# A fifth room for raw expert weights, and a first norm whose sums come from the residual operation and from ScalarE

## Chip, cores and metric

The kernel runs on one core of a Trainium2 chip. The metric is device time in microseconds (us) of one execution; the time of a kernel is the median of its runs. An execution was also taken by the hardware profiler, and the rows below are from it. DVE is VectorE, ACT is ScalarE, POOL is GpSimd, PE is TensorE's matmul, PEld its weight load, SP the SyncE queue that issues most transfers.

## What is computed

One layer of a decoder over 2048 tokens of width 1024. The part that matters here:

```
x = layer_norm(ALPHA * x + g1 * (mixed @ w_out), ln_mix_g, ln_mix_b)      # the first norm
h = x * (1 + sc2) + sh2
scores = sigmoid(h @ router_w); 8 of 64 experts are chosen for each token
y = sum over the chosen experts e of gate * (silu(h @ w1[e]) * (h @ w3[e])) @ w2[e]  + a shared expert
x = layer_norm(ALPHA * x + g2 * y, ln_ffn_g, ln_ffn_b)
layer_norm: (x - mean) * rsqrt(mean((x - mean)^2) + 1e-5) * g + b
```

`mixed` is made by three token mixers (a recurrent one and two kinds of attention) that take the first half of the time.

## The kernel before, in words

The program is written as tiles in pools. A pool has a number of rooms (`bufs`) for each tile name; a tile that is made when all rooms are taken waits until the oldest one's last reader is done. The order of the instructions on each engine is fixed when the program is built, by a scheduler that goes by the order in the source, by priorities and by its own planned times; on the chip each engine's queue runs in that order, and semaphores hold an instruction until what it needs is there.

**Phase C (`phase_c`, the first norm and the routing).** 16 blocks of 128 tokens go through `tile_`. For each block the mixed rows are multiplied by w_out in two halves of 512 columns (48 matmuls, L1836). DVE adds the residual (`scalar_tensor_tensor`, L1837) into `r` and takes statistics of each half (`bn_stats`, L1840). `layer_norm_hat` joins them (`bn_aggr`, L1996), adds the epsilon (L1998), takes the reciprocal root in eleven small DVE operations (L711 to L716), makes the bias (L2001), and ACT writes the normalised rows (L2004). DVE then makes `h2` (L1845) and `h2p` (L1849, read by PE for the router, L1860 and L1865) and the scaled rows that are kept (L1851, L1852). `route` works out the chosen experts of four or two blocks at a time, on DVE, in pieces put between the blocks; after the last block `rank_experts` sorts the experts by their load.

**Experts (`moe_phase`).** Work goes unit by unit: three units of the shared expert, then the 64 experts in the order largest, smallest, second largest and so on, each in groups of up to 320 tokens, then the shared expert again with the second norm. Expert weights come in as six raw tiles `wraw` of 128x1024 (512 KB each) an expert: SP loads one into a room of pool `e_wr` (four rooms, L2055), ACT copies it to the high part (L2059), DVE subtracts to get the low part (L2060), which frees the room. High and low parts lie in ten rooms of 8 KB (`e_ws`). PE runs the hidden matmuls (L2093 for small groups, L2112 for large ones), the way back (L2129), transposes of the gathered tokens (L2072) and small matmuls that find token numbers (L2194). These last two share three PSUM rooms named `tr` (L2072's are freed by L65, L2194's by the small DVE operations L2202 and L2203, and the transposes of L2103 in small groups by L65 again). POOL gathers tokens (L2140) and adds results to memory (L2166) by indirect transfers.

Of the kernel before, what the change touches and what calls it, by code (L numbers as in the profile page):

```python
# [6 lines left out]
F32 = mybir.dt.float32  # L7
# [5 lines left out]
AF = mybir.ActivationFunctionType  # L13
ALU = mybir.AluOpType
AX = mybir.AxisListType
PSUM = bass.MemoryType.PSUM
P = 128
T = 2048
D = 1024
# [9 lines left out]
ALPHA = 2.0 ** 0.25  # L29
# [673 lines left out]
def rsqrt(nc, pool, x, shape, floor=None, name="rs"):  # L703

    V = nc.vector
    if floor is not None:
        V.tensor_scalar(x, x, floor, None, op0=ALU.max)
    t = pool.tile(shape, I32, name=name + "i")
    y = pool.tile(shape, F32, name=name + "y")
    a = pool.tile(shape, F32, name=name + "a")  # L710
    V.tensor_scalar(t, x.bitcast(I32), 1, None, op0=ALU.logical_shift_right)  # L711
    V.tensor_scalar(y.bitcast(I32), t, -1.0, float(0x5f3759df), op0=ALU.mult, op1=ALU.add)  # L712
    for _ in range(3):
        V.scalar_tensor_tensor(a, y, -0.5, y, op0=ALU.mult, op1=ALU.mult)  # L714
        V.tensor_tensor(a, a, x, op=ALU.mult)  # L715
        V.scalar_tensor_tensor(y, a, 1.5, y, op0=ALU.add, op1=ALU.mult)  # L716
    return y
# [848 lines left out]
def mixed(nc, S, pool, t, res, queue, lo_eng):  # L1566

    m = pool.tile([P, KT, P], F32, name="m")
    queue.dma_start(m, S["mixT"].rearrange("(k p) t -> p k t", p=P)[:, :, t * P:(t + 1) * P])
    yield  # L1570
    mH = pool.tile([P, KT, P], F32R, name="mH")
    mL = pool.tile([P, KT, P], F32R, name="mL")
    split_to(nc, mH, mL, m, lo_eng=lo_eng)
    res += [mH, mL]
    yield
# [179 lines left out]
def phase_c(tc, A, g, S, mixT, modrow, C):  # L1755


    nc = tc.nc
    V, G, ACT, PE = nc.vector, nc.gpsimd, nc.scalar, nc.tensor
    woH, woL = C.wo  # L1760
    with ExitStack() as es:
# [3 lines left out]
        wk = pool("c_wk", 2)  # L1765
# [13 lines left out]
        sm = pool("c_sm", 1)  # L1779
# [36 lines left out]
        mv = mixT.rearrange("(k p) t -> p k t", p=P)  # L1816

        def tile_(t, h2T):
            t0 = t * P
            parts = C.first if t == 0 else []  # L1820
            load = mixed(nc, S, mx_ if t % 2 else C.mx, t, parts, G if t == 1 else nc.sync, V)
            if t:
                next(load)
            x = xp.tile([P, D], F32, name="x")
            nc.sync.dma_start(x, A["x"][0, t0:t0 + P, :])
            if t:
                next(load)
            mH, mL = parts
            yield
            r = rp.tile([P, D], F32, name="r")  # L1830
            for n in range(2):
                ps = C.pp.tile([P, CH], F32, name="po")
                sl = slice(n * 512, (n + 1) * 512)
                for k in range(KT):
                    for i, (a_, b_) in enumerate(((mH, woH), (mH, woL), (mL, woH))):
                        PE.matmul(ps, lhsT=a_[:, k, :], rhs=b_[:, k, sl], start=(k == 0 and i == 0), stop=(k == KT - 1 and i == 2))  # L1836
                V.scalar_tensor_tensor(r[:, sl], x[:, sl], ALPHA, ps, op0=ALU.mult, op1=ALU.add)  # L1837
                if n == 0:
                    st = sm.tile([P, 2, 6], F32, name="lnst", bufs=2)
                V.bn_stats(out=st[:, n, :], in_=r[:, sl])  # L1840
                yield
            xh = layer_norm_hat(tc, sm, r, r, st=st)
            yield
            h2 = wk.tile([P, D], F32, name="h2")
            V.tensor_tensor(h2, xh, bc["sc2"], op=ALU.mult)  # L1845

            hp = wk.tile([P, D], F32, name="h2p", bufs=3)
            cut = lambda a: a.rearrange("p (q k) -> p q k", k=KT)
            V.tensor_tensor(hp.rearrange("p (k q) -> p q k", k=KT), cut(h2), cut(bc["sh2"]), op=ALU.add)  # L1849
            h2 = hp  # L1850
            V.tensor_tensor(xh, xh, lng, op=ALU.mult)  # L1851
            V.tensor_tensor(xh, xh, lnb, op=ALU.add)  # L1852
            nc.sync.dma_start(S["x1"][t0:t0 + P, :], xh)
            nc.sync.dma_start(S["h2"][t0:t0 + P, 0:D], h2)
            yield
            hT = wk.tile([P, KT, P], F32, name="hT")
            for n in range(2):
                ps = pt.tile([P, CH], F32, name="tr")
                for k in range(4):
                    PE.transpose(ps[:, k * P:(k + 1) * P], h2[:, (4 * n + k) * P:(4 * n + k + 1) * P], g.ident)  # L1860
                ACT.activation(hT[:, 4 * n:4 * n + 4, :].rearrange("p a b -> p (a b)"), ps, AF.Copy)
            yield
            ps = pr.tile([P, CH], F32, name="rt")
            for k in range(KT):
                PE.matmul(ps[:, 0:NE], lhsT=hT[:, k, :], rhs=rw[:, k, :], start=(k == 0), stop=(k == KT - 1))  # L1865
            ACT.activation(h2T, ps[:, 0:NE], AF.Sigmoid)
            yield
# [80 lines left out]
        for t in range(NT + 2):  # L1948
            if t < NT:
                if t in starts:  # L1950
                    scs[t] = sm.tile([P, TPC, NE], F32, name="sc", bufs=2)[:, 0:starts[t]]
                    first = t
                live[t] = tile_(t, scs[first][:, t - first, :])
                next(live[t])
# [30 lines left out]
        rank_experts(tc, g, S, cnt_e, sm, pr)  # L1985


def layer_norm_hat(tc, sm, out, r, parts=1, st=None):

    nc = tc.nc  # L1990
    if st is None:
        st = sm.tile([P, 2, 6], F32, name="lnst")
        for n in range(2):
            nc.vector.bn_stats(out=st[:, n, :], in_=r[:, n * 512:(n + 1) * 512])
    mv = sm.tile([P, 2], F32, name="lnmv")
    nc.vector.bn_aggr(out=mv, in_=st)  # L1996
    va = sm.tile([P, 1], F32, name="lnva")
    nc.vector.tensor_scalar(va, mv[:, 1:2], 1e-5, None, op0=ALU.add)  # L1998
    y = rsqrt(nc, sm, va, [P, 1], None, "ln")
    nb = sm.tile([P, 1], F32, name="lnnb")  # L2000
    nc.vector.scalar_tensor_tensor(nb, mv[:, 0:1], -1.0, y, op0=ALU.mult, op1=ALU.mult)  # L2001
    for i in range(parts):
        c = slice(i * D // parts, (i + 1) * D // parts)
        nc.scalar.activation(out[:, c], r[:, c], AF.Identity, bias=nb, scale=y)  # L2004
    return out
NEAR = 4
NEAR2 = 5
# [6 lines left out]
def moe_phase(tc, A, g, S, modrow, out):  # L2014
    nc = tc.nc
    V, G, ACT, PE = nc.vector, nc.gpsimd, nc.scalar, nc.tensor
    with ExitStack() as es:
        pool = lambda name, bufs, **k: es.enter_context(tc.tile_pool(reuse_waits="tile", name=name, bufs=bufs, **k))
        permI, perm = g.permI, g.perm
        right = lambda name, bufs: es.enter_context(tc.tile_pool(reuse_waits="tile", side="right", name=name, bufs=bufs))  # L2020

        wr = right("e_wr", 4)
        hp = right("e_h", 2)
        xg = right("e_x", 6)
        cs = right("e_const", 1)
# [3 lines left out]
        sm = pool("e_sm", 3)  # L2029
# [269 lines left out]
        bufs = []  # L2299
# [158 lines left out]
def layer(tc, A, S, out):  # L2458
    g = Ctx()
    with ExitStack() as est:  # L2460
        setup(tc, A, g, est)
        moe_consts(tc, g, est)
        mod_params(tc, A, g)
        mod_first(tc, A, g)
        g.kes = ExitStack()
        g.kp = g.kes.enter_context(tc.tile_pool(reuse_waits="tile", name="fixed", bufs=1))
        phase_a1(tc, A, g, S)
        with ExitStack() as esC:
            C = mixers(tc, A, g, S, S["mixT"], S["modrow"], esC)
            phase_c(tc, A, g, S, S["mixT"], S["modrow"], C)  # L2470
        moe_phase(tc, A, g, S, S["modrow"], out)
# [22 lines left out]
```

## Time and profile before

| what | value |
|---|---|
| median of 3 runs | 3736.85 us (3732.08 to 3749.77) |
| the profiled execution | 3729.63 us, span from first to last instruction 3727.9 us |
| mean granted TensorE clock | 0.969 of 2.4 GHz |
| busy share of the span: PE, PEld, DVE, ACT, POOL | 92%, 80%, 71%, 53%, 24% |

The stages that the change touches are phase C, from about 1801 to 2072 us, and the experts, from 2072 us to the end. A row of the timeline has the start, the length, the engine, the line, the operation, the output and input tiles with their shapes, the number of instructions merged, and in brackets the idle time of the engine before it with what ended it. A row of the waits has the waiting engine and line, what it waited for, the total in us, how often, and the longest. In the windows each engine has its busy time and the number of instructions, and behind them stand the granted clock, the share of time in which the 16 DMA engines were busy, and GB/s.

### The profile page before, as it was taken

To read this page: it belongs to the slowest core of one execution; us is meant where nothing else is said; L and a number is where in the kernel's file an instruction comes from. 1 tells how busy PE (TensorE), PEld (TensorE's weight loads), DVE (VectorE), ACT (ScalarE), POOL (GpSimd) and SP (SyncE) were. 2 spreads that over 40 slices of the span, in tenths; PEclk is the share of its full clock that TensorE was granted. 3 is DMA by queue.
4 is the path that set the end of the run, shared out by engine and by line. 5 is a ranking of instruction groups with operands and counts; after the bars stand their busy time and mean duration, and the time that the engine had idled before them with its cause. 6 is when DMAs were issued, how large, how long until landed. Compare 5 with 4: busy or idle time off the path is not lost. (4 is left out here: it accounts for less than half of the span.)

```text
span 3727.9 us, 64046 instructions
## 1 busy us (share of the span) xinstructions
PE 3439.3 (92%) x23084; PEld 2985.7 (80%) x23084; DVE 2640.9 (71%) x6951; ACT 1962.2 (53%) x3471; POOL 881.8 (24%) x817
## 2 busy tenths in 40 slices
PE   7899999799999879999898799999999999999998
PEld 5677777688888767778787798998888888888996
DVE  6555899888888678888799545555556555556659
ACT  4243656355555567767322355555555555556642
POOL 1000000322223155543000022332223322232210
PEclk9999999899999889999999899999999999999999
DMA  7756466400000132222543478888889888888986
GB/s 251 232 199 221 150 211 226 162 26 25 20 24 18 30 105 79 84 66 78 170 149 140 146 206 232 242 232 233 244 244 242 244 236 234 236 234 256 290 237 215
DMA packets 276235, 640.38 MB, mean 172 GB/s; under 512 B 34428, under 2 KB 115364, under 8 KB 275784
## 3 DMA queue, kind: packets, MB, share of 16 engines
q1 hardware_dynamic: 231760, 481.09, 38.6%
q0 software_dynamic: 40832, 150.32, 18.2%
q10 hardware_dynamic: 3320, 4.83, 0.4%
q8 instruction: 183, 3.00, 0.3%
q14 instruction: 140, 1.15, 0.1%
HBM read 467.14 MB, written 169.00 MB: 171 GB/s over the span
## 5 line engine op out<-in xcount | busy, mean ns | idle before, releaser
L2112 PE MATMUL p<-hH,w 128*128 128x256 f32 (+8 forms) x4352 | 875.1, 289 | 9.3 <-DVE w L2060 6.6
L2112 PEld LDWEIGHTS p<-hH,w 128*128 128x128 f32 x4352 | 707.4, 191 | 18.9 <-DVE w L2060 6.9
L2060 DVE TENSOR_TENSOR w<-wraw,w 128x1024 fp32r<-128x1024 f32 x396 | 474.7, 1223 | 293.2 <-ACT w L2059 278.9
L2112 PE MATMUL p<-hL,w 128*128 128x256 f32 (+8 forms) x2176 | 617.2, 284 | 0.7 <-DVE hL L65 0.7
L2059 ACT ACTIVATE w<-wraw 128x1024 fp32r<-128x1024 f32 x396 | 406.2, 1054 | 234.5 <-DMA wraw<-in_exp_w_dram 112.2
L2166 POOL DMA_INDIRECT scratch_acc<-y,idx x157 | 262.3, 1671 | 782.6 <-ACT y L2165 312.8
L2129 PE MATMUL py<-w,gH 128*128 128x512 f32 (+5 forms) x1384 | 441.8, 401 | 2.0 <-ACT gH L62 1.6
L2112 PEld LDWEIGHTS p<-hL,w 128*128 128x128 f32 x2176 | 416.4, 191 | 6.5 <-DVE hL L65 0.9
L343 PE MATMUL pj<-hTH,w 128*128 128x512 f32 x1152 | 376.6, 402 | 16.6 <-ACT w L202 10.8
L65 DVE TENSOR_TENSOR hL<-tr,hH 128x512 fp32r<-128x512 f32 (+7 forms) x346 | 213.2, 627 | 210.8 <-ACT hH L62 197.6
L2129 PEld LDWEIGHTS py<-w,gH 128*128 128x128 f32 (+5 forms) x1384 | 236.6, 178 | 68.4 <-issue 8.1
L2165 ACT ACTIVATE y<-py,gt 128x512 f32<-128x512 f32 (+5 forms) x314 | 213.6, 683 | 145.9 <-PE py L2129 132.8
L343 PEld LDWEIGHTS pj<-hTH,w 128*128 128x128 f32 x1152 | 220.5, 193 | 70.8 <-ACT w L202 13.8
L62 ACT ACTIVATE hH<-tr 128x512 fp32r<-128x512 f32 (+7 forms) x346 | 184.3, 545 | 176.1 <-PE tr L2072 156.5
L2129 PE MATMUL py<-w,gL 128*128 128x512 f32 (+5 forms) x692 | 273.9, 396 | 0.6 <-DVE gL L65 0.5
L2140 POOL DMA_INDIRECT x<-scratch_h,idx x157 | 162.9, 1038 | 333.0 <-DVE L L2182 80.3
L343 PE MATMUL pj<-hTL,w 128*128 128x512 f32 x576 | 230.9, 401 | 0.0
L2072 PE MATMUL tr<-ident,x 128*128 128x128 f32 (+5 forms) x1384 | 191.9, 265 | 35.0 <-issue 17.9
L2072 PEld LDWEIGHTS tr<-ident,x 128*128 128x128 f32 (+5 forms) x1384 | 149.6, 140 | 46.0 <-issue 30.5
L2129 PEld LDWEIGHTS py<-w,gL 128*128 128x128 f32 (+5 forms) x692 | 122.9, 178 | 39.1 <-DVE gL L65 1.8
L2093 PE MATMUL p<-w,hH 128*128 128x256 f32 (+2 forms) x736 | 141.8, 289 | 0.0
L343 PEld LDWEIGHTS pj<-hTL,w 128*128 128x128 f32 x576 | 111.5, 194 | 23.5 <-issue 0.9
(626 smaller groups left out, 8152.0 us busy)
## 6 DMA issues: line engine op xcount, KB each, us to landing
wraw<-in_exp_w_dram SPq DMA_DIRECT2D x384, 512.0 KB
w<-scratch_wH SPq DMA_DIRECT2D x57, 512.0 KB
w<-scratch_wL SPq DMA_DIRECT2D x57, 512.0 KB
mw<-in_w_mod_dram SPq DMA_DIRECT2D x48, 512.0 KB
scratch_rw<-po SPq DMA_DIRECT2D x44, 256.0 KB
w<-in_w_in_dram SPq DMA_DIRECT2D x21, 512.0 KB
x<-in_x_dram SPq DMA_DIRECT2D x40, 256.0 KB
scratch_wH<-w SPq DMA_DIRECT2D x19, 512.0 KB
```

Source lines behind the costliest of these rows:

```text
L62: nc.scalar.activation(hi, src, AF.Copy)
L65: (lo_eng or nc.vector).tensor_tensor(lo, src, hi.bitcast(F32), op=ALU.subtract)
L343: nc.tensor.matmul(ps, lhsT=a_[:, k, :], rhs=b_[k], start=(k == 0 and i == 0), stop=(k == KT - 1 and i == 2))
L2059: ACT.activation(wh[:, c], raw, AF.Copy)
L2060: V.tensor_tensor(wl[:, c], raw, wh[:, c].bitcast(F32), op=ALU.subtract)
L2072: PE.transpose(ps[:, k * n:(k + 1) * n], x[0:n, (4 * h + k) * P:(4 * h + k + 1) * P], g.ident[0:n, 0:n])
L2093: PE.matmul(ps[i][:n, 0:256], lhsT=(hH, hL)[a][:, k, 0:n], rhs=w[i][b][:, k, :], start=(k == 0 and j == 0), stop=(k == KT - 1 and j == 2))
L2112: PE.matmul(ps[i][:, 0:n], lhsT=w[i][a][:, k, m * P:(m + 1) * P], rhs=(hH, hL)[b][:, k, 0:n], start=(k == 0 and j == 0), stop=(k == KT - 1 ...
L2129: PE.matmul(ps[:n], lhsT=(gH, gL)[a][:, m, c:c + n], rhs=w[2][b][:, m, h * CH:(h + 1) * CH], start=(more is None and m == 0 and j == 0), s ...
L2140: G.indirect_dma_start(out=x[0:m, :], out_offset=None, in_=S["h2"], in_offset=bass.IndirectOffsetOnAxis(ap=ix[0:m], axis=0))
L2165: ACT.activation(y[:m, hs], ps[:m], AF.Copy, scale=gt[:m])
L2166: G.indirect_dma_start(out=S["acc"], out_offset=bass.IndirectOffsetOnAxis(ap=ix[0:m], axis=0), in_=y[0:m, :], in_offset=None, compute_op=A ...
```

## The change

It does three things. The pool `e_wr` gets a fifth room. In the first norm the residual operation also writes the sum of each half (`accum_out`), and `bn_stats` and `bn_aggr` go. The mean is made from the two sums, ACT squares the centred rows with an accumulated sum (into the memory of `h2`, which is thrown away and written again later), and DVE turns that sum into the variance plus epsilon. The sign of `mean` is negative in the new code, so the bias is a plain product.

```diff
-                V.scalar_tensor_tensor(r[:, sl], x[:, sl], ALPHA, ps, op0=ALU.mult, op1=ALU.add)
                 if n == 0:
-                    st = sm.tile([P, 2, 6], F32, name="lnst", bufs=2)
-                V.bn_stats(out=st[:, n, :], in_=r[:, sl])
+                    su = sm.tile([P, 2], F32, name="lnsu", bufs=2)
+                V.scalar_tensor_tensor(r[:, sl], x[:, sl], ALPHA, ps, op0=ALU.mult, op1=ALU.add, accum_out=su[:, n:n + 1])
                 yield
-            xh = layer_norm_hat(tc, sm, r, r, st=st)
-            yield
             h2 = wk.tile([P, D], F32, name="h2")
+            xh = layer_norm_hat(tc, sm, r, r, su, h2)
+            yield
...
-def layer_norm_hat(tc, sm, out, r, parts=1, st=None):
+def layer_norm_hat(tc, sm, out, r, su, junk):
...
-    mv = sm.tile([P, 2], F32, name="lnmv")
-    nc.vector.bn_aggr(out=mv, in_=st)
+    mean = sm.tile([P, 1], F32, name="lnmean")
+    nc.vector.tensor_scalar(mean, su[:, 0:1], su[:, 1:2], -1.0 / D, op0=ALU.add, op1=ALU.mult)
     va = sm.tile([P, 1], F32, name="lnva")
-    nc.vector.tensor_scalar(va, mv[:, 1:2], 1e-5, None, op0=ALU.add)
+    nc.scalar.activation(junk, r, AF.Square, bias=mean, accum_out=va)
+    nc.vector.tensor_scalar(va, va, 1.0 / D, 1e-5, op0=ALU.mult, op1=ALU.add)
     y = rsqrt(nc, sm, va, [P, 1], None, "ln")
     nb = sm.tile([P, 1], F32, name="lnnb")
-    nc.vector.scalar_tensor_tensor(nb, mv[:, 0:1], -1.0, y, op0=ALU.mult, op1=ALU.mult)
-    for i in range(parts):
-        c = slice(i * D // parts, (i + 1) * D // parts)
-        nc.scalar.activation(out[:, c], r[:, c], AF.Identity, bias=nb, scale=y)
+    nc.vector.tensor_tensor(nb, mean, y, op=ALU.mult)
+    nc.scalar.activation(out, r, AF.Identity, bias=nb, scale=y)
     return out
...
-        wr = right("e_wr", 4)
+        wr = right("e_wr", 5)
```

## Rows read from the trace of the kernel before

**Rows 1.** The page's first part: busy time of each engine, share of the span, instructions.

```profile
PE 3439.3 (92%) x23084; PEld 2985.7 (80%) x23084; DVE 2640.9 (71%) x6951; ACT 1962.2 (53%) x3471; POOL 881.8 (24%) x817
```

**Rows 2.** Windows of phase C: one before PE's last w_out matmul, and the stretch from that matmul to the experts (busy us of PE, PEld, DVE, ACT, POOL; granted clock; DMA share; GB/s).

```profile
1960.00:2000.00 40.00, 40.00 (x216) 34.10 (x215) 37.34 (x121) 10.28 (x15) 1.34 (x2) 1.00 0.39 136
...
2018.00:2072.00 54.00, 22.54 (x127) 18.52 (x125) 46.28 (x193) 13.77 (x21) 5.59 (x10) 0.67 0.33 115
```

**Rows 3.** Windows of the experts, with the same columns.

```profile
2200.00:2700.00 500.00, 488.67 (x3617) 450.53 (x3616) 277.44 (x646) 277.02 (x436) 147.32 (x108) 1.00 0.85 231
2700.00:3400.00 700.00, 671.10 (x4698) 606.53 (x4697) 407.70 (x940) 396.74 (x620) 205.17 (x151) 0.99 0.86 239
3400.00:3600.00 200.00, 200.00 (x1454) 187.15 (x1453) 126.21 (x245) 123.45 (x190) 49.83 (x36) 1.00 0.96 282
```

**Rows 4.** What PE waited for from 2200 to 2700 us (total us, times, longest).

```profile
PE tr L2194 <- DVE L L2182: 7.8, 7, 1.1
PE tr L2072 <- DVE cj L2202: 1.9, 3, 1.0
```

**Rows 5.** The same from 2700 to 3400 us.

```profile
PE tr L2072 <- issue: 17.9, 9, 2.6
PE tr L2072 <- DVE cj L2202: 8.9, 3, 3.6
PE tr L2072 <- PE p L2112: 1.4, 2, 0.8
```

**Rows 6.** Timeline of PE, the end of one such wait.

```profile
2772.76 0.57 PE L2072 MATMUL tr<-ident,x 112*128 112x112 f32 x4 [3.60 <-DVE cj L2202]
```

**Rows 7.** Timeline of DVE in the same place.

```profile
2771.05 1.23 DVE L2060 TENSOR_TENSOR w<-wraw,w 128x1024 fp32r<-128x1024 f32 x1 [4.49 <-ACT w L2059]
...
2772.53 0.23 DVE L2202 TENSOR_SCALAR_CACHE_REDUCE cj<-tr,pos 128x16 f32<-128x16 f32 x1
```

**Rows 8.** Timeline of ACT in the same place.

```profile
2764.61 0.67 ACT L2165 ACTIVATE y<-py,gt 128x512 f32<-128x512 f32 x1
2769.97 1.06 ACT L2059 ACTIVATE w<-wraw 128x1024 fp32r<-128x1024 f32 x1 [4.68 <-DMA wraw<-in_exp_w_dram]
```

**Rows 9.** Timeline of SP's queue before it: the times at which raw loads are issued.

```profile
2755.60 0.33 SPq L2055 DMA_DIRECT2D wraw<-in_exp_w_dram  x1
...
2761.30 13.14 SPq L2055 DMA_DIRECT2D wraw<-in_exp_w_dram  x6
```

**Rows 10.** Timeline of POOL before it.

```profile
2760.47 1.67 POOL L2140 DMA_INDIRECT x<-scratch_h,idx  x1 [0.30 <-issue]
```

**Rows 11.** Waits from 2700 to 3400 us of ACT for raw loads, and of SP's queue for rooms.

```profile
ACT w L2059 <- DMA wraw<-in_exp_w_dram: 63.4, 35, 5.8
...
SPq L2055 <- DVE w L2060: 426.0, 99, 15.1
```

**Rows 12.** Timeline of ACT at another wait of PE (one that ended at 3160.80 us after 2.38 us).

```profile
3155.06 1.06 ACT L2059 ACTIVATE w<-wraw 128x1024 fp32r<-128x1024 f32 x1 [1.14 <-DMA wraw<-in_exp_w_dram]
3158.04 1.06 ACT L2059 ACTIVATE w<-wraw 128x1024 fp32r<-128x1024 f32 x1 [1.57 <-DMA wraw<-in_exp_w_dram]
```

**Rows 13.** Timeline of DVE in the same place, and PE's row behind it.

```profile
3156.15 1.23 DVE L2060 TENSOR_TENSOR w<-wraw,w 128x1024 fp32r<-128x1024 f32 x1 [0.49 <-ACT w L2059]
...
3159.13 1.23 DVE L2060 TENSOR_TENSOR w<-wraw,w 128x1024 fp32r<-128x1024 f32 x1 [1.36 <-ACT w L2059]
...
3160.80 0.63 PE L2072 MATMUL tr<-ident,x 128*128 128x128 f32 x4 [2.38 <-issue]
```

**Rows 14.** Windows of 5 us at the first and the last of the five places between 2200 and 3400 us where the granted clock falls; all five show 0.66.

```profile
2729.00:2734.00 5.00, 4.69 (x22) 4.42 (x23) 3.36 (x13) 2.31 (x4) 1.27 (x1) 0.66 0.89 198
...
3292.00:3297.00 5.00, 4.39 (x15) 3.63 (x16) 3.22 (x13) 1.29 (x2) 1.97 (x2) 0.66 1.01 315
```

**Rows 15.** Instructions of single lines (count, then shortest/median/longest in ns, first and last start): the two that go (L1840, L1996), and, from the second norm, the ones that come (L2371's read of the accumulator, L2327, L2329).

```profile
L1840 DVE BATCH_NORM_STATS2 lnst<-r x32: 672/686/696, 1809.2 to 2024.3; 128x6 f32<-128x512 f32 x32
...
L1996 DVE BATCH_NORM_AGGREGATE lnmv<-lnst x16: 186/203/209, 1810.6 to 2026.0; 128x2 f32<-128x12 f32 x16
...
L2371 DVE DVE_READ_ACCUMULATOR w<-py,x x20: 81/82/88, 3625.5 to 3716.9; 128x1 f32 x20
...
L2327 DVE TENSOR_SCALAR lnmean<-lnsu x16: 200/207/214, 3625.5 to 3717.0; 128x1 f32<-128x1 f32 x16
...
L2329 ACT ACTIVATE x<-w,lnmean x16: 1132/1148/1155, 3625.8 to 3717.3; 128x1024 f32<-128x1024 f32 x16
L2329 ACT ACTIVATION_READ_ACCUMULATOR x<-w,lnmean x16: 181/186/189, 3626.8 to 3718.4; 128x1 f32 x16
```

**Rows 16.** Timeline of DVE after PE's last w_out matmul: the last block's residual, the first wait, and the first subtraction for the experts.

```profile
2020.79 0.68 DVE L1837 SCALAR_TENSOR_TENSOR r<-x,po 128x512 f32<-128x512 f32 x1
...
2033.94 0.29 DVE L1888 TENSOR_TENSOR gt<-gs 128x128 f32<-128x128 f32 x1 [2.58 <-DMA scratch_h<-gt]
...
2070.93 4.63 DVE L2060 TENSOR_TENSOR w<-wraw,w 128x1024 fp32r<-128x1024 f32 x4
```

**Rows 17.** Timeline of PE where the experts begin.

```profile
2072.21 0.79 PE L2112 MATMUL p<-hH,w 128*128 128x256 f32 x2 [6.60 <-DVE w L2060]
```

**Rows 18.** Groups of ACT by line: squares of the recurrent mixer, and the one table load of phase C (busy us, mean ns of one, idle before).

```profile
L839 ACT ACTIVATE sq<-kk 128x512 f32<-128x512 f32 x12 | 7.6, 632 | 5.2 <-DVE kk L911 5.2
...
L1866 ACT ACT_TABLE_LOAD x1 | 1.3, 1283 | 0.0
```

More of the change, by code (lines that the diff above doesn't have):

```diff
@@ L1836, in tile_ @@
                         PE.matmul(ps, lhsT=a_[:, k, :], rhs=b_[:, k, sl], start=(k == 0 and i == 0), stop=(k == KT - 1 and i == 2))
-                V.scalar_tensor_tensor(r[:, sl], x[:, sl], ALPHA, ps, op0=ALU.mult, op1=ALU.add)
                 if n == 0:
-                    st = sm.tile([P, 2, 6], F32, name="lnst", bufs=2)
-                V.bn_stats(out=st[:, n, :], in_=r[:, sl])
+                    su = sm.tile([P, 2], F32, name="lnsu", bufs=2)
+                V.scalar_tensor_tensor(r[:, sl], x[:, sl], ALPHA, ps, op0=ALU.mult, op1=ALU.add, accum_out=su[:, n:n + 1])
                 yield
-            xh = layer_norm_hat(tc, sm, r, r, st=st)
+            h2 = wk.tile([P, D], F32, name="h2")
+            xh = layer_norm_hat(tc, sm, r, r, su, h2)
             yield
-            h2 = wk.tile([P, D], F32, name="h2")
             V.tensor_tensor(h2, xh, bc["sc2"], op=ALU.mult)
@@ L1985, in phase_c @@
         rank_experts(tc, g, S, cnt_e, sm, pr)
-def layer_norm_hat(tc, sm, out, r, parts=1, st=None):
+def layer_norm_hat(tc, sm, out, r, su, junk):
     nc = tc.nc
[L1991 to L1994, printed above, removed]
-    mv = sm.tile([P, 2], F32, name="lnmv")
-    nc.vector.bn_aggr(out=mv, in_=st)
+    mean = sm.tile([P, 1], F32, name="lnmean")
+    nc.vector.tensor_scalar(mean, su[:, 0:1], su[:, 1:2], -1.0 / D, op0=ALU.add, op1=ALU.mult)
     va = sm.tile([P, 1], F32, name="lnva")
-    nc.vector.tensor_scalar(va, mv[:, 1:2], 1e-5, None, op0=ALU.add)
+    nc.scalar.activation(junk, r, AF.Square, bias=mean, accum_out=va)
+    nc.vector.tensor_scalar(va, va, 1.0 / D, 1e-5, op0=ALU.mult, op1=ALU.add)
     y = rsqrt(nc, sm, va, [P, 1], None, "ln")
     nb = sm.tile([P, 1], F32, name="lnnb")
-    nc.vector.scalar_tensor_tensor(nb, mv[:, 0:1], -1.0, y, op0=ALU.mult, op1=ALU.mult)
-    for i in range(parts):
-        c = slice(i * D // parts, (i + 1) * D // parts)
-        nc.scalar.activation(out[:, c], r[:, c], AF.Identity, bias=nb, scale=y)
+    nc.vector.tensor_tensor(nb, mean, y, op=ALU.mult)
+    nc.scalar.activation(out, r, AF.Identity, bias=nb, scale=y)
     return out
```

## Prediction, made before the changed kernel was run

> **What bounds the kernel now.** I read the page's busy shares first, then windows stage by stage, then the waits of the engine that is full, and last the timeline of single waits. PE is busy for 92% of the span [rows 1], so a gain has to be a stretch in which PE stands still. In the experts PE is close to full: 488.67 of 500 us, 671.10 of 700 and 200 of 200 [rows 3]. It stands still for about 11 us from 2200 to 2700, for 29 us from 2700 to 3400, and not at all after that. The other place is the end of phase C: from 2018 to 2072 PE works 22.54 of 54 us, while DVE works 46.28 [rows 2].
>
> The waits name what PE stands still for. Up to 2700 it is mostly the small matmul L2194, 1.1 us seven times, held by L2182 on DVE [rows 4]. From 2700 on it is the transposes of the gathered tokens (L2072): 17.9 + 8.9 + 1.4 = 28.2 us in 14 waits, all but two of them over 1 us [rows 5]. These transposes need one of three PSUM rooms, and small DVE operations free these rooms.
>
> One of the waits, read backwards, shows why that is late. PE starts at 2772.76 after 3.60 us, behind the operation cj on DVE [rows 6]. In DVE's queue cj stands behind a weight subtraction that waited 4.49 us for ACT's copy [rows 7]. ACT's copy waited 4.68 us for a raw weight load [rows 8]. SP issued that load at 2761.30 [rows 9]; it took 8.7 us to be usable, and a gather started on POOL at 2760.47 [rows 10]. SP's queue spends 426 us of these 700 waiting for subtractions, which are what frees a room, and ACT waits 63.4 us for raw loads in 35 waits [rows 11]. So a lack of rooms makes loads late, and the lateness reaches PE through two in-order queues.
>
> **The change, part by part.**
>
> *The fifth room.* With five rooms a load takes the release before the one it takes now. The load issued at 2761.30 could have gone at 2755.60, when the one before it went [rows 9]: 5.7 us earlier. Its wait was 4.68 us [rows 8], and ACT was busy to 2765.28 anyway, so that wait goes if the transfer takes the same 8.7 us. The second load of a pair gains less, because the releases of a pair are one subtraction apart, about 1.2 us [rows 7]. That matters in the other kind of wait, where two copies come late, by 1.14 and 1.57 us [rows 12]; DVE loses 0.49 + 1.36 us there, out of PE's 2.38 us [rows 13]. The first goes whole; of the second about 0.4 us stays, so 1.45 of 2.38, or 60%, is won.
>
> Taken over all: the three waits marked cj go whole, 8.9 us. Of the nine marked "issue", 17.9 us in all, I take 65%, a little above the one worked out since many have only one late copy: 11.6 us. Together 20.5 us. The bounds are 0 (every transfer takes the longer for being issued earlier) and 28.2 + 1.9 = 30.1 us [rows 4, 5]. The 7.8 us of L2194 stay: I find no late load in front of them.
>
> *The clock.* At five places behind such waits the granted clock is 0.66 over 5 us [rows 14]: part of that stretch is at 1.2 GHz, after PE stood still (for 3.60 us at one of them, [rows 6]). Each costs 0.34 x 5 = 1.7 us, 8.5 us in all. If the waits shrink under about 1.5 us, most of the falls go: I take 6 us, between 0 and 8.5.
>
> *The sums of the first norm.* For each block DVE loses two bn_stats and one bn_aggr, 2 x 0.686 + 0.203 = 1.575 us, and gains two reads of the accumulator and the mean, 2 x 0.082 + 0.207 = 0.371 us [rows 15], so 1.2 us less. The epsilon, the root and the bias keep their counts. ACT gains 1.148 + 0.186 = 1.33 us [rows 15] and is busy 10.28 of 40 us there [rows 2]. Up to 2018 PE is full, so nothing of this is seen; that cover is gone only behind PE's last w_out matmul. There the last block's residual is at 2020.79, DVE's first wait ends at 2033.94, and DVE reaches the experts' subtractions at 2070.93 [rows 16], for which PE waits until 2072.21 [rows 17]. Until that wait DVE's queue runs full, and it carries the norms of the last two to three blocks, so I count its queue as 2 to 3 us shorter there. Against that stands a longer chain: the last bn_stats and bn_aggr (0.89 us) give way to a read, the mean, the square and its read (1.62 us), 0.73 us more for each block whose chain is waited for, and DVE's queue now waits at the variance until ACT has squared. I take 2 us less. The ends are 5 us less and 4 us more; the reordering of some 190 DVE operations in that stretch is why they lie so far apart.
>
> The Trainium skill (ScalarE: Activation LUTs, "Rules for kernel authors") speaks against this part: additions and products belong on VectorE rather than ScalarE. By that rule alone the 0.73 us would be all that the part does, at most 16 x 0.73 = 12 us slower. The rows show the other side, DVE at 37.34 of 40 us and ACT at 10.28 [rows 2], so the sum goes by the queue that is full.
>
> *What is moved.* The claim on `h2` comes earlier, at the square. It has two rooms and its last reader is h2p of two blocks before, so nothing waits. The fifth room lets one more of the shared expert's loads go early in phase C; PE needs the first of those weights at 2072.21 [rows 17], so this is covered even if the memory came free late. At the end the second norm's two rows take two of five rooms instead of four, and PE waits for no weights there.
>
> Sum against the profiled execution of 3729.63 us: 20.5 + 6 + 2 = 28.5 us less, 3701.1 us. The median shown is 7.2 us above that execution, so I forecast 3708.
>
> **The rivals.**
>
> *The transfers are the limit, not the room.* DMA is busy 0.86 of the time from 2700 to 3400 [rows 3], and the slow load ran beside a gather [rows 10]. Then an earlier issue lengthens the transfer, and the wait moves to the second copy of the pair, which gains 1.2 us at best. Against it: the first load would go 5.7 us earlier, before the gather at 2760.47, and from 3400 to 3600 the engines reach 0.96 [rows 3], so there is room. The Trainium skill (DMA: Bandwidth & Descriptors, "Issuing engines are not separate DMA queues") says that transfers from SP and POOL share the same 16 engines and interleave; that is what this rival needs. Each of the 14 waits then loses some 0.7 us, 10 us, with 2 us of the norm: 3725.
>
> *Squares reload ACT's tables.* ACT loads a table once in phase C, at the sigmoid [rows 18]. If the square were not in that set, each block would load twice, 2 x 1.283 us. The steady part hides it (10.28 of 40 us busy), the last two blocks show 5 us more, and with the longer chain the norm part costs 7 us instead of winning 2: 3717. Against it: squares in the recurrent mixer have no load of their own [rows 18]. The Trainium skill (ScalarE: Activation LUTs, "Table sets: the hidden batching unit") lists copy and identity as in every set and not the square; no run here shows the sigmoid set with a square.
>
> *Slower: the new order.* The queues' order is planned when the program is built. With a room more the planner can put conversions earlier in DVE's queue, ahead of the small operations that free PSUM, where they wait for a place among the weights rather than for a load. The waits at L2182 are of about that price, 1.1 us [rows 4]. Two in each of the 32 pairs of experts would be 70 us in place of 7.8, and with the 28.5 us won the time would be 3771. It turns slower than the measurement tells from about 43 new waits on.
>
> **How the numbers follow.** Some 0.5%, 19 us, is about what a measurement of this kernel can tell from no change; 3718 is the line. The forecast has 0.58, and all but 0.04 of it lies under 3718; its own range is 3693 (all waits and clock falls gone, 5 us at the end of phase C) to 3722. The transfer limit has 0.28, the tables 0.05 (0.01 of it under the line), the new order 0.06, and 0.03 is left for a longer end of phase C that eats half of the gain, within 0.5%. Faster is 0.54 + 0.01 = 0.55; slower 0.06; same is the rest, 0.39. The range runs from 3690 to 3736: it takes in the transfer limit and leaves out the slower case and some 0.1 at the two edges.
>
> **What would show it.** In the changed profile PE's waits at L2072 from 2700 to 3400 should fall from 28 to about 8 us, ACT's waits for raw loads from 63 to under 25, and the granted clock should be 1.00 at four of the five places. L2194's waits should stay near 8 us. In phase C DVE should be some 19 us less busy, ACT 21 us more, with one table load, and PE's first expert matmuls should come 54 us or less after the last of w_out. The prediction is wrong if ACT's waits for loads stay at 50 us or more, if they fall and PE's waits do not, or if the stretch from 2018 to 2072 grows by over 5 us.

## The result, and the profile after

The changed kernel takes 3689.24 us (median of 4 runs, 3682.48 to 3697.16), the kernel before 3737.24 beside it: ratio 0.9875, 95% interval 0.9856 to 0.9894, 48 us less. I had forecast 28.5 us less, 3708; the time lies 0.8 us under the lower end of my range.

The two profiled executions are 32.4 us apart (3729.63 and 3697.16), less than the medians. The reason is code that the change does not touch, the part ahead of phase C, which took 11.2 us longer in the second. From the start to the first w_out matmul it takes 1743.1 to 1765.5 us over the fourteen profiled executions of this text, with PE's instructions in the same order. So stages are compared, each from a PE instruction to a PE instruction (us):

| stage | before | after | difference |
|---|---|---|---|
| start to first w_out matmul (untouched) | 1750.1 | 1761.2 | +11.2 |
| first to last w_out matmul | 268.5 | 268.4 | 0 |
| last w_out matmul to the experts' running matmuls ("end of phase C") | 55.5 | 48.4 | -7.1 |
| from there to the last hidden matmul ("experts") | 1608.0 | 1571.5 | -36.5 |
| the rest | 45.9 | 45.9 | 0 |

The experts' running matmuls are taken from 2074.07 and 2078.11 us on, just behind PE's last wait for a weight. Without the untouched part that is 43.6 us less.

The end of phase C as a window, moved by the 11 us that it starts later [rows 2], and the experts in the windows of [rows 3]:

```profile
2029.00:2083.00 54.00, 27.50 (x163) 23.61 (x162) 46.84 (x186) 15.27 (x24) 3.81 (x6) 0.68 0.41 133
2200.00:2700.00 500.00, 491.08 (x3647) 454.33 (x3646) 277.67 (x648) 280.90 (x439) 150.40 (x108) 1.00 0.85 235
2700.00:3400.00 700.00, 693.13 (x4912) 628.23 (x4911) 425.05 (x986) 416.56 (x649) 215.43 (x159) 1.00 0.88 252
3400.00:3600.00 200.00, 197.74 (x1407) 183.02 (x1406) 121.29 (x225) 114.52 (x177) 46.78 (x30) 0.99 0.89 262
```

The first window holds the experts' first 5 us too, since they begin earlier in it. From 2700 to 3400 PE's missing 29 us have become 7, at a granted clock of 1.00, and the DMA engines move 252 instead of 239 GB/s. What PE waits for from 2200 to 2700, and below it from 2700 to 3400 (L2188 was L2194, L2066 was L2072, L2106 was L2112; answers to [rows 4, 5]):

```profile
PE tr L2188 <- DVE L L2176: 7.8, 7, 1.2
PE tr L2066 <- DVE hL L65: 1.1, 1, 1.1
```

```profile
PE tr L2066 <- PE p L2106: 4.8, 10, 0.5
PE tr L2066 <- issue: 1.4, 1, 1.4
PE p L2106 <- DVE hL L65: 0.7, 1, 0.7
```

The waits of the transposes fell from 28.2 to 6.2 us, and those behind `cj` are gone. The seven waits of 1.1 us stay. Over the whole of the experts, as the table cuts them, before and after:

```profile
2074.07:3682.03 1607.96, 1555.47 (x11113) 1421.90 (x11112) 935.63 (x2121) 881.48 (x1388) 425.22 (x314) 0.99 0.85 238
```

```profile
2078.11:3649.58 1571.47, 1546.86 (x11112) 1416.88 (x11112) 933.47 (x2121) 885.16 (x1387) 432.20 (x314) 1.00 0.85 244
```

So of the 36.5 us, 27.9 are time in which PE stood still (52.5 and 24.6 us), and 8.6 are PE's busy time. ACT's waits for raw loads from 2700 to 3400, 63.4 us before [rows 11]:

```profile
ACT w L2053 <- DMA wraw<-in_exp_w_dram: 16.0, 11, 3.1
```

The place of [rows 6 to 9] shows how. SP's queue issues the load of that role (the 169th) at 2751.25, 7.9 us before the subtraction ahead of it starts (2759.13), where it was 3.9 us (2761.30 and 2765.19). That is 4.0 us earlier, where I had worked out 5.7: a small load of token counts (`cw`) stands in front of it in SP's queue, at 2750.66. It is enough. ACT's copy of it finds the data there, right behind `y`, and PE comes to the transposes without a wait. First the timeline of SP's queue, then ACT's, then PE's:

```profile
2748.41 0.33 SPq L2049 DMA_DIRECT2D wraw<-in_exp_w_dram  x1
2750.66 0.33 SPq L2166 DMA_DIRECT2D cw<-scratch_cum  x1
2751.25 5.45 SPq L2049 DMA_DIRECT2D wraw<-in_exp_w_dram  x3
```

```profile
2758.55 0.67 ACT L2159 ACTIVATE y<-py,gt 128x512 f32<-128x512 f32 x1
2759.27 1.06 ACT L2053 ACTIVATE w<-wraw 128x1024 fp32r<-128x1024 f32 x1
```

```profile
2761.11 0.55 PE L2066 MATMUL tr<-ident,x 112*128 112x112 f32 x4
```

In phase C ACT squares 16 blocks, with one table load at the sigmoid as before [rows 18]; groups of ACT by line (busy us, mean ns of one, idle before):

```profile
L1993 ACT ACTIVATE h<-r,lnmean 128x1024 f32<-128x1024 f32 x16 | 18.4, 1152 | 26.5 <-DVE lnmean L1991 26.5
...
L1993 ACT ACTIVATION_READ_ACCUMULATOR h<-r,lnmean 128x1 f32 x16 | 3.0, 185 | 0.0
L1865 ACT ACT_TABLE_LOAD x1 | 1.3, 1283 | 0.0
```

From the first w_out matmul to DVE's first subtraction for the experts ACT is busy 119.9 us where it was 98.8, the 21 us more that I wanted, and DVE 264.8 where it was 280.7, 16 us less where I wanted some 19.

At its end DVE no longer waits for the gate's transfer at the comparison `gt`, where it had waited 2.58 us with the last block's `h` right behind [rows 16]:

```profile
2032.05 0.67 DVE L1839 SCALAR_TENSOR_TENSOR r<-x,po 128x512 f32<-128x512 f32 x1
...
2038.32 0.16 DVE L1997 TENSOR_TENSOR lnnb<-lnmean,lny 128x1 f32<-128x1 f32 x1
2038.42 0.29 DVE L1887 TENSOR_TENSOR gt<-gs 128x128 f32<-128x128 f32 x1
...
2039.83 1.23 DVE L1844 TENSOR_TENSOR h<-r,bcsc 128x1024 f32<-128x1024 f32 x1
```

### The profile page after: what moved, and what is told of

It is laid out like the page before. It is cut to its first block, busy times and chain, and to the rows that moved or that the text cites. A ratio compares the mean times of both kernels' runs of the same rounds, so it can differ in the third digit from the quotient of the medians.

```text
span 3695.4 us, 64069 instructions
## 1 busy us (share of the span) xinstructions
PE 3428.6 (93%) x23084; PEld 2981.0 (81%) x23084; DVE 2625.1 (71%) x6951; ACT 1987.6 (54%) x3503; POOL 887.7 (24%) x817
## 3 DMA queue, kind: packets, MB, share of 16 engines
q14 instruction: 140, 1.15, 0.1%
## 5 line engine op out<-in xcount | busy, mean ns | idle before, releaser
L2106 PE MATMUL p<-hH,w 128*128 128x256 f32 (+8 forms) x4352 | 872.8, 288 | 9.4 <-DVE w L2054 6.6
L2106 PEld LDWEIGHTS p<-hH,w 128*128 128x128 f32 x4352 | 705.1, 191 | 18.8 <-DVE w L2054 6.9
L2106 PE MATMUL p<-hL,w 128*128 128x256 f32 (+8 forms) x2176 | 616.1, 283 | 0.7 <-DVE hL L65 0.7
L2160 POOL DMA_INDIRECT scratch_acc<-y,idx x157 | 269.7, 1718 | 782.6 <-ACT y L2159 282.0
L2106 PEld LDWEIGHTS p<-hL,w 128*128 128x128 f32 x2176 | 415.1, 191 | 6.6 <-DVE hL L65 0.9
L65 DVE TENSOR_TENSOR hL<-tr,hH 128x512 fp32r<-128x512 f32 (+7 forms) x346 | 213.1, 627 | 212.7 <-ACT hH L62 211.7
L2066 PE MATMUL tr<-ident,x 128*128 128x128 f32 (+5 forms) x1384 | 191.8, 265 | 9.5 <-PE p L2106 4.8
L2066 PEld LDWEIGHTS tr<-ident,x 128*128 128x128 f32 (+5 forms) x1384 | 150.5, 141 | 18.7 <-PE p L2106 6.3
L2112 DVE TENSOR_TENSOR s<-s,p 128x256 f32<-128x256 f32 (+8 forms) x136 | 55.6, 409 | 130.5 <-PE p L2106 125.6
```

Of the source, the lines that this page charges most:

```text
L65: (lo_eng or nc.vector).tensor_tensor(lo, src, hi.bitcast(F32), op=ALU.subtract)
L2066: PE.transpose(ps[:, k * n:(k + 1) * n], x[0:n, (4 * h + k) * P:(4 * h + k + 1) * P], g.ident[0:n, 0:n])
L2106: PE.matmul(ps[i][:, 0:n], lhsT=w[i][a][:, k, m * P:(m + 1) * P], rhs=(hH, hL)[b][:, k, 0:n], start=(k == 0 and j == 0), stop=(k == KT - 1 ...
L2160: G.indirect_dma_start(out=S["acc"], out_offset=bass.IndirectOffsetOnAxis(ap=ix[0:m], axis=0), in_=y[0:m, :], in_offset=None, compute_op=A ...
```

## The experiments

Each ran beside the kernel before on the same chip. "End of phase C" and "experts" are the stages of the table above, from the profile of each.

**The fifth room alone.**

```diff
-        wr = right("e_wr", 4)
+        wr = right("e_wr", 5)
```

> Only the fifth room; the first norm is the old one. The instructions of PE and POOL stand in the same order as in the kernel before, and in the experts DVE, ACT and SP differ in the last six units alone. Theory A (rooms free too late): all of the gain in the experts is here without the norm. From the experts' running matmuls to the last hidden matmul it takes 1572 us instead of 1608 (PE's gaps 25 instead of 53 us, no fall of the clock in that stretch), the end of phase C stays at 55 us, and the whole is some 36 us faster, ratio 0.990. Rival B (transfers are the limit): ACT's waits for raw loads stay over 50 us from 2700 to 3400 and under 10 us are won. Rival C (the experts gain because phase C ends otherwise, with five weights converted early): the experts' stretch stays near 1600 us.

Measured: ratio 0.9901 (0.9876 to 0.9926), 37 us; experts 1571.4, end of phase C 56.2 us. PE's waits from 2700 to 3400:

```profile
PE tr L2072 <- PE p L2112: 5.6, 11, 0.8
PE p L2112 <- DVE hL L65: 0.7, 1, 0.7
```

Theory A holds, and B and C fall: the room alone gives what the experts gained, with PE's and POOL's instructions in the same order as before, and ACT's waits for raw loads from 2700 to 3400 are 5.0 us. One fall of the clock (a stretch at the lower of TensorE's two levels, 1.2 GHz) is left in the experts, 1.7 us, where I wanted none.

**The new norm alone** (the changed kernel with four rooms).

```diff
-        wr = right("e_wr", 5)
+        wr = right("e_wr", 4)
```

> Only the new first norm; four rooms as before. Theory A: from the last matmul of w_out to the experts' running matmuls it takes 48 us instead of 55, the experts stay at 1608 us with their waits and five falls of the clock, and the whole is 7 us faster, ratio 0.998. By my forecast's size of this part it would be 2 us, 53 us for that stretch. Rival C (the five rooms' earlier loads are what shortens the end of phase C): that stretch stays at 54 to 56 us.

Measured: 0.997 (0.9953 to 0.9986); end of phase C 48.6, experts 1601.7 us. PE's waits from 2700 to 3400 are of the old kind:

```profile
PE tr L2066 <- issue: 16.6, 9, 2.4
PE tr L2066 <- DVE cj L2196: 3.8, 3, 1.5
```

In the experts the clock falls four times where I wanted five (3.41 us at half the clock each, 6.8 us in all). So the two parts add up: 56.2 and 48.6 us at the end of phase C, each with its own norm. The 7 us are the norm's, more than three times what I had counted.

**Three rooms.**

```diff
-        wr = right("e_wr", 4)
+        wr = right("e_wr", 3)
```

> The kernel before with three rooms instead of four: the dose in the other direction. Theory A: each load goes at least one release later, the waits of the transposes grow and more of the small matmuls get such waits; going from five to four rooms cost 36 us in the experts, so going to three costs 60 to 150 us, and ACT's waits for raw loads from 2700 to 3400 rise from 63 to over 150 us. Rival B (transfers are the limit): 0 to 15 us.

Measured: 1.0157 (1.0118 to 1.0196), 59 us slower; experts 1670.0 us, with 87.0 us in which PE stands still (52.5 with four rooms) and sixteen falls of the clock instead of five. ACT from 2700 to 3400:

```profile
ACT w L2059 <- DMA wraw<-in_exp_w_dram: 128.0, 69, 5.6
```

The direction is that of theory A, and B is out by far. The 62 us in the experts are at the lower end of my 60 to 150, and ACT's waits are 128 us where I wanted over 150. Three, four and five rooms: 1670, 1608 and 1571 us.

**The old statistics put back, unread.** The new norm with four rooms, and

```diff
+                if n == 0:
+                    st = sm.tile([P, 2, 6], F32, name="lnst", bufs=2)
+                V.bn_stats(out=st[:, n, :], in_=r[:, sl])
```

> The new first norm with four rooms, and the old two bn_stats of each block put back on DVE with nobody reading them: 2 x 0.69 us more on DVE for each of 16 blocks, ACT and the chain as in the new norm. Theory A (the end of phase C is as long as DVE's queue of its last two to three blocks): the stretch behind the last w_out matmul is 2.7 to 4.1 us longer than without them, so 51 to 52 us; the blocks before are hidden by PE. Rival D (what counts is the new order of the small operations, not their time): the stretch stays at 48 to 49 us. Rival E (DVE's whole queue of phase C counts): 22 us longer.

Measured: 1.0008 (0.999 to 1.0027); end of phase C 55.9 us. All 7.3 us are back, more than A's 2.7 to 4.1 and far less than E's 22. D's 48 to 49 us are out; but the order came back with the load (the last gate operation is behind the last residual again, 8.5 us after the last w_out matmul, where the new norm alone has it 2.9 us before), so this run does not part the two. The timeline of DVE shows what A had left out, the gate's transfer:

```profile
2032.49 0.15 DVE L2000 TENSOR_TENSOR lnnb<-lnmean,lny 128x1 f32<-128x1 f32 x1
...
2036.75 0.29 DVE L1890 TENSOR_TENSOR gt<-gs 128x128 f32<-128x128 f32 x1 [2.93 <-DMA scratch_h<-gt]
2036.96 1.22 DVE L1847 TENSOR_TENSOR h<-r,bcsc 128x1024 f32<-128x1024 f32 x1
```

Against the new norm alone, the last block's bias (`lnnb`) comes 2.7 us later after the last w_out matmul (11.5 and 8.8 us), as A had it; `h` follows it 2.9 us later, and the router 1.6 us later than that. The experts took 1619.3 us here, where four rooms gave 1608.0 and 1601.7; the norm's two kernels of four rooms differ there by 17.6 us with the same kinds of wait (see the last heading).

**A room of its own for the gates** (kernel before).

```diff
-            gate = sm.tile([P, TPC, NE], F32, name="gt")[:, 0:B]
+            gate = sm.tile([P, TPC, NE], F32, name="gate")[:, 0:B]
```

> The kernel before (old norm, four rooms) with a room of its own for the gate tile, which shared one with the comparisons of the next set of blocks. The last comparison of phase C then has no transfer to wait for: DVE's wait of 2.58 us in front of it goes, and h of the last block stands right behind it. Theory F (part of what the new norm won at the end of phase C is this wait): h can move up until ACT's Identity is done, some 2 us, so the stretch from the last w_out matmul to the experts' running matmuls goes from 55.5 to 53.5 us and the whole is 2 us faster, ratio 0.9995. Rival (the wait was filled, other work on DVE takes the place): 55 to 56 us.

Measured: 0.9994 (0.9977 to 1.0011), which tells nothing by itself; end of phase C 53.8 instead of 55.5 us. The timeline of DVE has `h` waiting for ACT now, and no more for a transfer:

```profile
2037.43 0.29 DVE L1888 TENSOR_TENSOR gt<-gs 128x128 f32<-128x128 f32 x1
...
2038.13 1.22 DVE L1845 TENSOR_TENSOR h<-r,bcsc 128x1024 f32<-128x1024 f32 x1 [0.42 <-ACT r L2004]
```

So the wait is worth 1.8 us of that stage, as theory F had it.

**The squares on DVE** (new norm, four rooms).

```diff
-    nc.scalar.activation(junk, r, AF.Square, bias=mean, accum_out=va)
+    nc.vector.scalar_tensor_tensor(junk, r, mean, r, op0=ALU.add, op1=ALU.mult, accum_out=va)
```

> The new norm with four rooms, but the squares with their sum are made by DVE instead of ACT (one operation of 128x1024, 1.2 us, and one read). DVE then has as much to do as with the old norm: less 1.58 us, plus 0.37 and 1.3 us a block. Theory A (DVE's queue sets the end of phase C): the stretch behind the last w_out matmul is back at 54 to 56 us, with a wait for the gate's transfer again, and the whole is as before, ratio 0.998 to 1.002. Rival D (the accumulated sum, which frees DVE early, and the new order are what counts): 48 to 50 us, ratio 0.997.

Measured: 1.0007 (0.9993 to 1.0021); end of phase C 55.4, experts 1605.7 us. Theory A: with DVE's load as before, the stage is as before, with a wait for the gate's transfer again (1.48 us) and the last gate operation behind the last residual again. The accumulated sums alone win nothing; moving work from DVE to ACT does.

**Six rooms, five for gathers.**

```diff
-        wr = right("e_wr", 5)
+        wr = right("e_wr", 6)
-        xg = right("e_x", 6)
+        xg = right("e_x", 5)
```

> The changed kernel with six rooms for raw loads, and five for gathered tokens instead of six, which gives the memory. Theory A: the five rooms have taken what there was. ACT's waits for raw loads go from 16 to under 8 us between 2700 and 3400, the experts stay at 1568 to 1575 us, the ratio at 0.987 as with five. Rival G (each room more wins): another 8 to 12 us in the experts. Rival H (the gathers need six rooms): transposes wait for gathers and the experts are over 1580 us.

Measured: 0.9881 (0.9859 to 0.9903), as with five. ACT has no waits for raw loads left among its waits from 2700 to 3400. The experts take 5.7 us less (1565.7) and the rest 10.2 us more (56.1), so nothing is won. I had not foreseen that trade, and what makes the rest longer was not looked into; this kernel also has a room less for gathers, and the two are not parted here. The experts lie under A's 1568 and gain less than G's 8 us: five rooms had taken nearly all that there was.

**An earlier comparison.** The changed kernel with

```diff
-                grp[r] = at, beyond_group(cums[r], at)
+                with tc.high_priority(400):
+                    grp[r] = at, beyond_group(cums[r], at)
```

> The changed kernel with a higher priority for the comparison L (and its cast) that the small matmuls with the token numbers wait for: seven waits of 1.1 us are the largest that five rooms leave. If they come only from the comparison's place behind two subtractions in DVE's queue, they go: PE's waits there fall from 7.8 to under 2 us, the experts from 1571 to 1565 us, the ratio to the kernel before 0.986 instead of 0.9875. If the new place makes others late, the waits move and the experts stay at 1571 us or more.

Measured: 0.9855 (0.9833 to 0.9877), overlapping the changed kernel's interval; experts 1571.7 us, and the seven waits stay at 7.8 us. A miss: the comparison still stands behind the two subtractions, so the priority did not move what it should.

**The changed kernel again, and two pieces of DVE's work given to POOL.** The edits of the last three kernels (both in the last):

```diff
-            V.tensor_tensor(xh, xh, lng, op=ALU.mult)
-            V.tensor_tensor(xh, xh, lnb, op=ALU.add)
+            W = G if t >= NT - 2 else V
+            W.tensor_tensor(xh, xh, lng, op=ALU.mult)
+            W.tensor_tensor(xh, xh, lnb, op=ALU.add)
...
-            tc.keep_in_program_order(V.tensor_copy(st, w[:, 17:18]))
+            tc.keep_in_program_order((G if first is None else V).tensor_copy(st, w[:, 17:18]))
...
-                V.tensor_scalar(L[:, 0:m], pl[:, 0:m], st, None, op0=ALU.is_ge)
+                G.tensor_scalar(L[:, 0:m], pl[:, 0:m], st, None, op0=ALU.is_ge)
```

> The changed kernel once more, beside the three that follow. Theory A: ratio 0.9875 to the kernel before, 48.5 us behind the last w_out matmul, 1571.5 us in the experts.

> The changed kernel with the scaling rows of the last two blocks (r times lng, r plus lnb: 4 x 1.21 us on DVE) given to POOL, which is idle there; nothing but a store waits for them. Theory A (the end of phase C is as long as DVE's queue): DVE has 4.9 us less in front of the last chain and of the last route, so the stretch behind the last w_out matmul falls from 48.5 to 44 to 46 us, ratio 0.9865. Rival D (order, not queue): 48 to 50 us. Rival P (POOL's transfers of gates and counts, which stand behind the scaling in its queue, come late, 2.0 to 2.4 us for each operation): over 50 us.

> The changed kernel with the comparison L (and its cast) on POOL instead of DVE, since a higher priority did not move it from behind the two subtractions that wait for ACT. If DVE's in-order queue is the whole cause of the seven waits of 1.1 us, they go: PE's waits there fall from 7.8 to under 2 us, the experts to 1564 us, ratio 0.9855. If POOL's queue (its additions to memory take 1.7 us each) delays the comparison, the waits stay or grow, and the experts are at 1571 us or more.

> Both of the last two edits in one kernel. If each does what it should by the theory of queues, the sum: 45 us behind the last w_out matmul, 1564 us in the experts, some 10 us under the changed kernel, ratio 0.9845. If neither does, as the changed kernel or slower.

Measured:

| kernel | ratio | end of phase C | experts |
|---|---|---|---|
| changed, again | 0.9879 (0.9857 to 0.9900) | 48.5 | 1571.2 |
| scaling on POOL | 0.9879 (0.9861 to 0.9897) | 50.4 | 1570.3 |
| comparison on POOL | 0.9876 (0.9858 to 0.9895) | 48.5 | 1565.5 |
| both | 0.9880 (0.9858 to 0.9902) | 50.2 | 1570.3 |

The scaling on POOL made the stage 1.9 us longer where theory A wanted it 2.5 to 4.5 us shorter; what the timelines show of it is under the last heading. Rival P has the size but not the reason: DVE waits for no transfer in that stretch. The comparison on POOL took the seven waits away (no L2188 row is left from 2200 to 2700):

```profile
PE tr L2066 <- DVE hL L65: 1.5, 4, 0.4
PE tr L2066 <- issue: 0.7, 2, 0.4
```

and the experts 5.7 us, as forecast, but the whole time does not tell it from the changed kernel, and with both edits two waits of 1.8 us came back behind POOL's comparison. No version beats the changed kernel by more than is uncertain.

## Why the prediction was right, and where its sizes were off

The mechanisms of the room and of the clock came as forecast, that of the norm only in part, and each of the three terms came out larger than its value (27.9 us for 20.5, 8.6 for 6, 7.1 for 2). That is why the time lies just under the range.

**The fifth room** (forecast 20.5 us, bounds 0 to 30.1). The mechanism is shown by the room alone and by the dose of three to five rooms. The transposes' waits that I had counted, from 2700 to 3400, fell by 22.0 us, 28.2 to 6.2. PE's idle time in the whole of the experts fell by 27.9 us, since my value counted nothing outside that stretch. Of the nine waits marked "issue", where I had left 35%, 6.3 us, one of 1.4 us stays; ten short ones behind PE's own matmuls (4.8 us) took the place of the others.

**The clock** (6 us, 0 to 8.5). All five places of [rows 14] are gone. One new fall stands at 3594 us, behind a wait of 2.26 us (the 0.99 in the window from 3400 to 3600), so 6.8 of 8.5 us are won. The waits of 1.1 to 1.4 us that are left have no fall behind them. PE's busy time fell by 8.6 us; the other 1.8 us I did not take apart.

**The first norm** (2 us less, ends 5 less and 4 more) is the term that was mis-sized: 7.1 us, outside its ends. The step that failed is "I count its queue as 2 to 3 us shorter", taken as all there is. That much is right: after the last w_out matmul (ending at 2018.54 and 2029.68) the last block's bias comes at 11.5 before and 8.6 us after, 2.9 us earlier. But two things stand behind it. The bias is not what `h` waited for: DVE stood 2.58 us at the comparison `gt`, for the transfer of the gates, which share the one room of that name with it. I had the row [rows 16] and read it only as the end of DVE's full queue. With a shorter queue the planner places the last gate operation ahead of the last residual, 3 us before the last w_out matmul ends and no longer 9 us after it, so the transfer is over in time. Of the 2.6 us by which `h` follows the bias sooner, the room for the gates alone wins 1.8. And the router's matmul of the last block stands in PE's queue behind the transposes of the shared expert's tokens and a matmul that needs `mb` from DVE; that stretch is 11.4 us before and 9.8 after, 1.6 us more. 2.9 + 2.6 + 1.6 = 7.1. Timelines of PE, before and after:

```profile
2037.53 1.94 PE L1860 MATMUL tr<-ident,h2p 128*128 128x128 f32 x8 [6.85 <-DVE h2p L1849]
...
2048.74 0.24 PE L1929 MATMUL rt<-utri,mb 128*64 128x128 bf16 x1 [0.26 <-DVE mb L1924]
2048.92 2.00 PE L1865 MATMUL rt<-rwt,hT 128*128 128x64 f32 x16
```

```profile
2043.14 1.94 PE L1859 MATMUL tr<-ident,h2p 128*128 128x128 f32 x8 [6.22 <-DVE h2p L1848]
...
2052.78 0.24 PE L1928 MATMUL rt<-utri,mb 128*64 128x128 bf16 x1
2052.96 2.00 PE L1864 MATMUL rt<-rwt,hT 128*128 128x64 f32 x16
```

The 0.73 us of a longer chain, which I had set against the gain, did not show: between the mean (2033.79) and the variance (2035.31) DVE works on the counts of earlier blocks and waits 0.11 us. The rule that additions and products belong on VectorE (the Trainium skill, ScalarE: Activation LUTs, "Rules for kernel authors") is not borne out in this stage, where DVE is the full engine: with the squares on DVE it is 55.4 us, with them on ACT 48.6 (both with four rooms).

**The rivals.** The transfers were not the limit: 252 GB/s where there had been 239, and the waits went. The squares load no table of their own: the one load of phase C is the sigmoid's, with squares before and after it. The new order took nothing in the experts; at the end of phase C it was part of the gain.

**The sum.** 27.9 + 8.6 + 7.1 = 43.6 us in the stages, 48 in the medians; the interval of the ratio is 7 us to either side.

The Trainium skill (Perfetto Trace Analysis, "Optimization Strategy") says that the same gap repeating on the engine that should be saturated can mean too few buffers. The trace agrees for the transposes' waits, 28.2 us with four rooms and 6.2 with five. The most regular gap of all had another cause: the seven waits of 1.10 to 1.15 us stayed with five and with six rooms for raw weights, and went when their comparison left DVE's queue.

## What to carry to other kernels

Where an engine waits at regular work, follow the wait through each in-order queue back to the first thing that was late; a buffer was missing here three queues away from the engine that stood still, and the fourth and the fifth room bought 62 and 37 us in the experts, while the sixth, taken from the gathers, bought 6 there and nothing in the whole. Where DVE's queue ends a stage, count what stands behind each of its instructions, transfers that hold a room included: 1.2 us less a block became 7 us. Compare stages from instruction to instruction, since untouched code moved by 22 us from one execution to the next.

## What the runs showed of the hardware that was not expected

**POOL's operations stop some of DVE's.** With the scaling on POOL, its product took 4.0 us beside DVE's `h2p` (the sum behind it 2.35), and DVE's small operations beside it grew: the f16 difference of 64x496 took 2.19 us where it takes 0.66 without, `sel` 2.40 (0.29) and `e` 1.63 (0.25). The timeline of POOL, and that of DVE, with the scaling on POOL:

```profile
2016.75 4.01 POOL L1851 TENSOR_TENSOR r<-r,lng 128x1024 f32<-128x1024 f32 x1 [1.27 <-DVE h L1844]
2020.83 2.35 POOL L1852 TENSOR_TENSOR r<-r,lnb 128x1024 f32<-128x1024 f32 x1
...
2029.12 3.95 POOL L1851 TENSOR_TENSOR r<-r,lng 128x1024 f32<-128x1024 f32 x1 [4.00 <-DVE grank L1894]
2033.15 2.35 POOL L1852 TENSOR_TENSOR r<-r,lnb 128x1024 f32<-128x1024 f32 x1
```

```profile
2021.53 2.19 DVE L1937 TENSOR_TENSOR cw<-cume 64x496 f16<-64x496 f32 x1
...
2029.07 1.90 DVE L1848 TENSOR_TENSOR h2p<-h,bcsh 128x1024 f32<-128x1024 f32 x1
2030.82 2.40 DVE L1896 TENSOR_TENSOR sel<-sel,grank 128x128 f32<-128x128 f32 x1
...
2033.92 1.63 DVE L1909 TENSOR_SCALAR e<-sel,v 128x64 f32<-128x64 f32 x1
```

`h2p`, which started first, kept its 1.90 us, and POOL's product was lengthened. DVE's 2.40 us end at 2033.2, where POOL's product does (2033.07), and `e` ends at 2035.55, where POOL's sum does (2035.50): each was held until then. The Trainium skill (SBUF — State Buffer, "Who interferes with whom") says that a DVE instruction with two inputs in SBUF, or in a mode that uses both ports, shuts out a POOL instruction that reads SBUF, or is shut out by it, for the whole instruction. The rows agree for the difference and `sel`, which have two inputs; for `e`, with one, they don't tell which case it is. So of the 4.9 us that the scaling took from DVE's queue, 1.5 + 2.1 + 1.4 = 5.0 us came back in these three.

The 1.9 us more of the stage do not come from there. The router's last scores (`sc`) are ready 25.2 us after the last w_out matmul, and 25.3 us in the changed kernel. Behind them DVE reaches the experts' first subtraction after 22.0 us instead of 20.0. The planner has put the transposes of the shared expert's last tokens behind the router's matmuls, and their four subtractions (L65, 0.67 us each) stand between the steps of the last route. This is read from the timelines; no run tests it. Timelines of ACT and of DVE with the scaling on POOL, then of ACT and of DVE in the changed kernel:

```profile
2042.45 0.23 ACT L1866 ACTIVATE sc<-rt 128x64 f32<-128x64 f32 x1 [1.00 <-PE rt L1865]
```

```profile
2045.20 0.67 DVE L65 TENSOR_TENSOR hL<-tr,hH 128x512 fp32r<-128x512 f32 x1
...
2064.45 4.63 DVE L2055 TENSOR_TENSOR w<-wraw,w 128x1024 fp32r<-128x1024 f32 x4
```

```profile
2054.99 0.23 ACT L1865 ACTIVATE sc<-rt 128x64 f32<-128x64 f32 x1 [2.92 <-PE rt L1864]
```

```profile
2074.96 2.36 DVE L2054 TENSOR_TENSOR w<-wraw,w 128x1024 fp32r<-128x1024 f32 x2
```

**Missing rooms make the time uneven.** With four rooms the experts took 1601.7 to 1619.3 us in five profiled executions. With five rooms they took 1570.3 to 1571.7 us in six, and 1565.5 in the seventh, which had the comparison alone on POOL. Of the 17.6 us between the ends with four rooms, 8.5 are time in which PE stood still (48.1 and 56.7 us) and 9.1 are PE's busy time, with four falls of the clock in the shorter and eight in the longer; with five rooms each of the seven has one fall.

**A comparison of f16 rows costs POOL 1.43 us and DVE 0.30** (means of 64); groups by line, POOL's with the comparison there, then DVE's of the changed kernel:

```profile
L2176 POOL TENSOR_SCALAR L<-pl,st 128x384 f16<-128x384 f16 (+5 forms) x64 | 91.3, 1426 | 6.0
```

```profile
L2176 DVE TENSOR_SCALAR L<-pl,st 128x384 f16<-128x384 f16 (+5 forms) x64 | 19.1, 298 | 1.5
```
